# The second norm's factors move from the token tiles to the diagonals of the matrices that transpose them

## The chip, the cores and the metric

The kernel runs on one core of a Trainium2 chip. The metric is the device time of one execution in microseconds (us); the profiler also records the span of an execution, from its first to its last instruction. Five engines work side by side, each through its own list of instructions in order: PE (the tensor engine: matrix products), DVE, ACT and POOL (element-wise work) and SP (which here only issues DMA transfers). They wait for each other through semaphores. PE reads its operands from the on-chip memory SBUF and writes to PSUM, a small memory of eight banks from which DVE and ACT read. In the profile a product has two rows: PEld loads the stationary operand, PE streams the moving one.

## The reference, cut to what matters

One layer over 2048 latent tokens of 1024 channels, with 256 context tokens. Before each of its two halves the tokens are normed and modulated:

```python
def rmsnorm(x, g):
    y = xf * lax.rsqrt(jnp.mean(xf * xf, axis=-1, keepdims=True) + EPS) * g
def modulate(h, shift, scale):
    return h * (1.0 + scale) + shift

hx = modulate(rmsnorm(x, norm1_g), mx[:, :, 0], mx[:, :, 1])     # first norm
ux = hx @ w_in                                                   # mixer: FNet and HGRN2 branches
yx = merge_branches(ux, hgrn_readout(ux, ox, ...), w_a, w_b, w_out)
x = x + mx[:, :, 2] * yx
h2 = modulate(rmsnorm(x, norm2_g), mx[:, :, 3], mx[:, :, 4])     # second norm
x = x + mx[:, :, 5] * conv_ffn(h2, ffn_up, conv_w, conv_b, ffn_down, rows, cols)
return rmsnorm(x, final_g)
```

The norm's factor, 1 over the root of the mean square, is one number per token. Gain, scale and shift are one number per channel.

## The kernel before, in words

**Tiling.** Tokens are worked in four blocks (n = 0 to 3) of 512, each as four tiles (i = 0 to 3) of 128 tokens on the partitions by 1024 channels. The matrix products want the channels on the partitions, so a normed block is transposed in eight pieces (k = 0 to 7) of 128 channels: for each piece four transposes of 128x128, one for each token tile, fill one PSUM tile `pt` of 128x512. That is a "group of four" in what follows. Products are made in fp32 accuracy from three fast ones: an operand is split in `hi` (rounded to the format fp32r) and `lo` (the rest), and L146 to L148 add hi*hi, hi*lo and lo*hi. A few products (the FNet transforms, the scans) take plain fp32 operands.

**The function that transposes.** `modulate_steps` (L432) goes through the pieces k. For each it issues the group of four on PE (L440), then three steps that empty the PSUM tile: DVE forms A*pt+B in `mt` (L442), ACT forms the same rounded to fp32r as `hi` (L443), and DVE or POOL subtracts them to give `lo` (L445). A and B hold gain, scale and shift per channel. It is called for the first norm (at the start, for four blocks of tokens and the context, which has two tiles) and for the second norm (blocks 0 to 3, called through `h2_block`). The PSUM tiles `pt` come from rotating buffers: six at the start (tags tp, at, o), two for blocks 0 to 2 of the second norm, four for block 3.

**The norm's factors.** ACT squares and sums a token tile (L423, L962), DVE makes the factor `rs` in a chain of ten tiny instructions (L964, L125 to L129), and then DVE multiplies the token tiles by it: in place, four instructions of 128x1024 (L429 at the start, L970 in `h2_block`). Block 2 of the second norm is different: its tokens have been written to DRAM and come back in pieces `xc` of four 128x128 tiles (`reload_steps`, L972), and DVE multiplies each piece (L988) before it is transposed.

**What goes on around the second norm (phase 2, L844).** For each block n, `branches` makes eight output tiles j: for each j twelve products (four k by three) with w_a, then twelve with w_b, each set in one of two PSUM buffers `pj`, which DVE multiplies by a gate tile `gt` (L898). The two are added (L901), rounded by ACT (L902), and the rest is taken by DVE (L905). `out_proj` multiplies by w_out and adds the residual (L951, L952), and `h2_block` prepares the second norm of this block. Its eight groups of transposes are handed over as a generator and issued in between the next block's `branches` (none behind the tiles j = 0 and 1, one behind each of the next four, two behind the last two), so that block n is transposed while block n+1 is merged. Block 3 has no next one: its transposes stand among the first products of the up-projection (phase 3, `z`, L146 to L148). The gate tiles come from DRAM by SP (L880) in five rotating buffers of 128x512, two for each j, loaded one j ahead.

**Phase 3 and the end.** 44 up-projections with a 3x3 convolution on DVE and POOL, then the down-projection by a seven-product scheme (L1147 to L1149). There `ss` is a small tile of sums for the final norm, and behind it in the same SBUF pool lie the tiles `w`, `r0` and `r1`, into which weights and activations stream.

**What sets the order.** The program is written with tiles and pools, and a scheduler orders the instructions of each engine at compile time with its own estimate of how long each one takes. So another kind of instruction can also shift its neighbours.

Of the kernel before, what the change touches and what calls it, by code (L numbers as in the profile page):

```python
# [17 lines left out]
F32 = mybir.dt.float32  # L18
# [8 lines left out]
P = 128  # L27
# [4 lines left out]
TB = 512  # L32
KD = D // P
# [3 lines left out]
MUL, ADD, SUB = ALU.mult, ALU.add, ALU.subtract  # L37
# [57 lines left out]
class Layer:  # L95
# [335 lines left out]

    def modulate_steps(self, pool, xs, A, B, hi, lo, tags, every, bufs=2, k0=0, nk=KD):  # L432

# [3 lines left out]
        for k in range(k0, k0 + nk):  # L437
            pt = self.ps.tile([P, TB], F32, name="pt", tag=tags[k % len(tags)])
            for i in range(n):
                nc.tensor.transpose(pt[:, i * P:(i + 1) * P], xs[i][:, (k - k0) * P:(k - k0 + 1) * P], self.eye)  # L440
            tmp = pool.tile([P, TB], F32, name="mt", tag="mt", bufs=bufs)
# [427 lines left out]
    def branches(self, p4, n, t_lo, t_hi, bg):  # L869
# [7 lines left out]
        def load_gates(j):  # L877
            gates[j] = [p4.tile([P, TB], F32, name=f"gt{b}", tag="gt", bufs=5) for b in range(2)]
            for b in range(2):
                nc.sync.dma_start(gates[j][b], (self.dGA if b == 0 else self.dGB)[j][n])  # L880
# [75 lines left out]
    def h2_block(self, p4, n, xs, slots, tags):  # L956
# [7 lines left out]
        nc.vector.tensor_scalar(vv, ss, 1.0 / D, EPS, op0=MUL, op1=ADD)  # L964
        rs = self.rsqrt(p4, vv, 4)
        hi, lo = self.h2[n] = [self.ph.tile([P, KD, TB], F32R, name=f"h2{n}{i}", tag=f"H{slots[i]}") for i in range(2)]
        if n == 2:
            return self.reload_steps(p4, rs, hi, lo, tags)
        for i in range(4):
            nc.vector.tensor_scalar(xs[i], xs[i], rs[:, i:i + 1], None, op0=MUL)  # L970
        return self.modulate_steps(self.p4b, xs, self.mod2_A, self.mod2_B, hi, lo, tags, 4)

    def reload_steps(self, p4, rs, hi, lo, tags):

# [10 lines left out]
        def steps():  # L985
            for k in range(KD):
                xc = pieces.pop(0)
                nc.vector.tensor_tensor(xc, xc, fap(rs, 0, [(1, 4), (0, P)]), op=MUL)  # L988
                xs = [xc[:, i, :] for i in range(4)]
                for _ in self.modulate_steps(self.p4b, xs, self.mod2_A, self.mod2_B, hi, lo, tags, 4, 2, k, 1):  # L990
                    pass
                if k + 2 < KD:
                    pieces.append(load(k + 2))
                yield
# [156 lines left out]
    def down(self, last, pools):  # L1151
# [4 lines left out]
        with ExitStack() as es:  # L1156
# [13 lines left out]
            fg = p6.tile([P, D], F32, name="fg")  # L1170
            ss = p6.tile([P, 2, 16], F32, name="ss")
            X = {}
# [127 lines left out]
```

## Time and profile before

| | us |
|---|---|
| median of three runs | 3076.26 |
| lowest, highest | 3072.92, 3078.34 |
| profiled execution, its own time | 3078.62 |
| profiled execution, its span | 3076.8 |
| PE busy (98% of the span) | 3017.8 |
| DVE busy (60%) | 1847.2 |
| POOL busy (35%) | 1065.1 |
| ACT busy (30%) | 923.0 |

Busy time counts each engine by itself. "Idle before" in the rows of a timeline is the time in which the engine had nothing running ahead of that instruction, with the instruction that ended the wait. Times in a timeline count from the span's start. A row of a timeline can hold several equal instructions (x4); its second number is the time from the first one's start to the last one's end. The granted clock (PEclk) is the share of full speed that the tensor engine was given in a stretch; over the whole profiled run it was 0.994.

### The profile page before, as it was taken

The page shows a single profiled execution, that of the slowest core. Times are in us where ns is not written, and L with a number is a line of the kernel's source. Part 1 is how long each engine was busy: PE and PEld are TensorE (multiplying, and loading weights), DVE is VectorE, ACT ScalarE, POOL GpSimd, SP SyncE. Part 2 cuts the span into 40 slices and gives each one's busy share as a digit, 9 for nine tenths or more (in the row PEclk, how much of TensorE's full clock was granted, in tenths as well). Part 3 has the DMA queues.
Part 4 walks back from the last instruction along what each step waited for, and adds up shares of the span by engine and source line. Part 5 has one row for each costly group of instructions (what it writes and reads, how often), then busy time and mean ns, then how long its engine had stood idle before and what let it go on. Part 6 is the DMA issues. An engine that isn't in the chain of part 4 may idle for free. (4 is left out here: it accounts for less than half of the span.)

```text
span 3076.8 us, 38641 instructions
## 1 busy us (share of the span) xinstructions
PE 3017.8 (98%) x14691; PEld 2507.9 (82%) x14691; DVE 1847.2 (60%) x2503; ACT 923.0 (30%) x1439; POOL 1065.1 (35%) x714
## 2 busy tenths in 40 slices
PE   8999999999999999999999999999999999999998
PEld 5977788888888888887777888888888888787876
DVE  6355544366666650256775777676767677664366
ACT  4322111233333331233443322333233323221122
POOL 2200101000000001234543566777677767401400
PEclk9999999999999999999999999999999999999999
DMA  6255555422333223555564344554455454898783
GB/s 251 86 170 175 183 170 162 149 93 94 102 107 102 94 76 103 177 190 189 186 210 136 118 140 142 166 172 163 148 164 180 145 162 163 309 389 283 226 304 133
DMA packets 314459, 516.25 MB, mean 168 GB/s; under 512 B 24267, under 2 KB 162338, under 8 KB 309922
## 3 DMA queue, kind: packets, MB, share of 16 engines
q1 hardware_dynamic: 289602, 428.77, 42.1%
q0 software_dynamic: 22368, 80.81, 7.5%
q10 hardware_dynamic: 2304, 4.20, 0.4%
q8 instruction: 116, 1.90, 0.3%
q14 instruction: 69, 0.57, 0.1%
HBM read 364.52 MB, written 149.16 MB: 167 GB/s over the span
## 5 line engine op out<-in xcount | busy, mean ns | idle before, releaser
L1062 DVE SCALAR_TENSOR_TENSOR ac<-z,cw,ac 128x1953 f32<-128x1953 f32 (+2 forms) x309 | 703.1, 2275 | 255.6 <-ACT be L1032 231.0
L146 PE MATMUL z<-h,w_up 128*128 128x512 f32 x1408 | 548.0, 389 | 0.0
L147 PE MATMUL z<-h,w_up 128*128 128x512 f32 x1408 | 548.0, 389 | 0.0
L148 PE MATMUL z<-h,w_up 128*128 128x512 f32 x1408 | 547.9, 389 | 0.0
L147 PEld LDWEIGHTS z<-h,w_up 128*128 128x128 f32 x1408 | 264.3, 188 | 54.9
L146 PEld LDWEIGHTS z<-h,w_up 128*128 128x128 f32 x1408 | 264.3, 188 | 54.7
L148 PEld LDWEIGHTS z<-h,w_up 128*128 128x128 f32 x1408 | 264.3, 188 | 54.7
L1037 POOL TENSOR_TENSOR ac<-ac,be 128x1984 f32<-128x1984 f32 x43 | 192.2, 4469 | 209.5 <-DVE ac L1062 209.4
L1029 ACT ACTIVATE ac<-z,vt,cw 128x2048 f32<-128x2048 f32 x44 | 90.9, 2067 | 454.4 <-PE z L148 454.4
L1147 PE MATMUL d<-w,g 128*128 128x512 f32 x528 | 209.5, 397 | 6.7 <-issue 3.0
L1149 PE MATMUL d<-w,g 128*128 128x512 f32 x528 | 208.4, 395 | 0.0
L1148 PE MATMUL d<-w,g 128*128 128x512 f32 x528 | 208.4, 395 | 0.0
L493 ACT ACTIVATE ev<-pj 128x512 f32<-128x512 f32 (+1 forms) x136 | 79.6, 585 | 369.1 <-PE pj L148 335.3
L102 ACT CAST g<-r 128x1024 fp32r<-128x1024 f32 x69 | 69.9, 1047 | 280.2 <-PE d L1149 113.3
L1136 POOL DMA_DIRECT2D w<-dW x69 | 37.4, 543 | 305.1 <-PE d L1149 275.3
L1138 DVE TENSOR_TENSOR r<-r,r 128x1024 f32<-128x1024 f32 x55 | 68.2, 1242 | 115.3 <-DMA r<-dZ 74.0
L787 PEld LDWEIGHTS pa<-bQ,bkc 128*128 128x128 f32 x896 | 120.6, 191 | 17.2 <-issue 10.8
L103 POOL TENSOR_TENSOR wab<-rw,wab 128x512 fp32r<-128x512 f32 x64 | 93.9, 1486 | 113.9 <-ACT wab L102 113.8
L787 PE MATMUL pa<-bQ,bkc 128*128 128x128 f32 x896 | 127.6, 286 | 1.3
L1147 PEld LDWEIGHTS d<-w,g 128*128 128x128 f32 x528 | 99.3, 188 | 35.0 <-DVE x L1214 6.8
L793 DVE COPY_PREDICATED bA<-mask,pa 128x512 f32<-128x512 uint8 x112 | 82.7, 738 | 71.6 <-PE pa L787 70.6
L781 ACT COPY bkc<-bK 128x512 f32<-128x512 f32 x112 | 74.2, 663 | 164.1 <-PE pa L787 95.2
(341 smaller groups left out, 6808.4 us busy)
## 6 DMA issues: line engine op xcount, KB each, us to landing
r<-dZ SPq DMA_DIRECT2D x124, 512.0 KB, 7.1
dW<-wsr POOLq DMA_DIRECT2D x77, 512.0 KB, 5.9
w<-dW POOLq DMA_DIRECT2D x69, 512.0 KB, 6.2
ws<-dV SPq DMA_DIRECT2D x132, 256.0 KB, 4.2
rw<-in_ffn_up_dram SPq DMA_DIRECT2D x88, 256.0 KB, 4.2
dZ<-ac SPq DMA_DIRECT2D x22, 1024.0 KB, 4.0
rw<-in_w_in_dram SPq DMA_DIRECT2D x72, 256.0 KB, 3.4
maw<-in_ada_w_dram SPq DMA_DIRECT2D x64, 256.0 KB, 3.1
```

The costliest lines, as they stand in the source:

```text
L103: (eng or self.nc.gpsimd).tensor_tensor(lo, raw, hi, op=SUB)
L146: self.nc.tensor.matmul(ps, lh, rh, start=start and i == 0, stop=False)
L147: self.nc.tensor.matmul(ps, lh, rl, start=False, stop=False)
L148: mm = self.nc.tensor.matmul(ps, ll, rh, start=False, stop=stop and i == last)
L787: mm = nc.tensor.matmul(pa[:, c], kc[:, c], fap(Q, w * P, [(2 * m, nw), (W + m, 2), (1, m)]), start=True, stop=True)
L793: v.copy_predicated(at.rearrange("p (w t) -> p w t", w=4), fap(self.mask, lv * P, [(0, 4), (1, P)]), pa.rearrange("p (w t) -> p w t", w=4))
L1029: self.centre = nc.scalar.activation(ac, z, AF.Identity, scale=self.cw[:, 4, jj:jj + 1], bias=self.v("cb", jj))
L1037: added = nc.gpsimd.tensor_tensor(ac[:, :SEQ - 64], ac[:, :SEQ - 64], be[:, 64:], op=ADD)
L1062: nc.vector.scalar_tensor_tensor(o, z3[:, r0 + dy:r1 + dy, c0 + dx:c1 + dx], self.cw[:, k, jj:jj + 1], o, op0=MUL, op1=ADD)
L1147: nc.tensor.matmul(acc, gh[:, t], wh, start=(k == 0), stop=False)
L1148: nc.tensor.matmul(acc, gh[:, t], wl, start=False, stop=False)
L1149: nc.tensor.matmul(acc, gl[:, t], wh, start=False, stop=(k == KH - 1))
```

## The change

For the second norm, the token tiles are no longer multiplied by the factors. Instead four diagonal matrices `dg` are made from the identity, one for each token tile, with the factors on the diagonal, and the step that transposes uses `dg` in the identity's place: the product of a tile (transposed) with a diagonal matrix is the transposed tile with each token's column scaled. [...] The buffer for `dg` (2 KB per partition) is taken from the gate tiles, which go from five buffers to four. The tile of sums `ss` of the end grows from 128 to 512 bytes per partition, with the same columns of it used.

```diff
--- before.py
+++ after.py
@@ -429,7 +429,7 @@
             nc.vector.tensor_scalar(xs[i], xs[i], rs[:, i:i + 1], None, op0=MUL)
         return xs
 
-    def modulate_steps(self, pool, xs, A, B, hi, lo, tags, every, bufs=2, k0=0, nk=KD):
+    def modulate_steps(self, pool, xs, A, B, hi, lo, tags, every, bufs=2, k0=0, nk=KD, dg=None):
 
 
         nc = self.nc
@@ -437,7 +437,8 @@
         for k in range(k0, k0 + nk):
             pt = self.ps.tile([P, TB], F32, name="pt", tag=tags[k % len(tags)])
             for i in range(n):
-                nc.tensor.transpose(pt[:, i * P:(i + 1) * P], xs[i][:, (k - k0) * P:(k - k0 + 1) * P], self.eye)
+                nc.tensor.matmul(pt[:, i * P:(i + 1) * P], xs[i][:, (k - k0) * P:(k - k0 + 1) * P],
+                                 dg[:, i, :] if dg else self.eye, start=True, stop=True)
             tmp = pool.tile([P, TB], F32, name="mt", tag="mt", bufs=bufs)
             nc.vector.tensor_scalar(tmp[:, :n * P], pt[:, :n * P], A[:, k:k + 1], B[:, k:k + 1], op0=MUL, op1=ADD)
             nc.scalar.activation(hi[:, k, :], pt[:, :n * P], AF.Identity, scale=A[:, k:k + 1], bias=B[:, k:k + 1])
@@ -875,7 +876,7 @@
         br, gates = self.br, {}
 
         def load_gates(j):
-            gates[j] = [p4.tile([P, TB], F32, name=f"gt{b}", tag="gt", bufs=5) for b in range(2)]
+            gates[j] = [p4.tile([P, TB], F32, name=f"gt{b}", tag="gt", bufs=4) for b in range(2)]
             for b in range(2):
                 nc.sync.dma_start(gates[j][b], (self.dGA if b == 0 else self.dGB)[j][n])
 
@@ -963,14 +964,15 @@
         vv = p4.tile([P, 4], F32, name="vv", tag="vv", bufs=2)
         nc.vector.tensor_scalar(vv, ss, 1.0 / D, EPS, op0=MUL, op1=ADD)
         rs = self.rsqrt(p4, vv, 4)
+        dg = p4.tile([P, 4, P], F32, name="dg", tag="dg", bufs=1)
+        for i in range(4):
+            nc.vector.tensor_scalar(dg[:, i, :], self.eye, rs[:, i:i + 1], None, op0=MUL)
         hi, lo = self.h2[n] = [self.ph.tile([P, KD, TB], F32R, name=f"h2{n}{i}", tag=f"H{slots[i]}") for i in range(2)]
         if n == 2:
-            return self.reload_steps(p4, rs, hi, lo, tags)
-        for i in range(4):
-            nc.vector.tensor_scalar(xs[i], xs[i], rs[:, i:i + 1], None, op0=MUL)
-        return self.modulate_steps(self.p4b, xs, self.mod2_A, self.mod2_B, hi, lo, tags, 4)
-
-    def reload_steps(self, p4, rs, hi, lo, tags):
+            return self.reload_steps(p4, dg, hi, lo, tags)
+        return self.modulate_steps(self.p4b, xs, self.mod2_A, self.mod2_B, hi, lo, tags, 4, dg=dg)
+
+    def reload_steps(self, p4, dg, hi, lo, tags):
 
         nc = self.nc
 
@@ -985,9 +987,8 @@
         def steps():
             for k in range(KD):
                 xc = pieces.pop(0)
-                nc.vector.tensor_tensor(xc, xc, fap(rs, 0, [(1, 4), (0, P)]), op=MUL)
                 xs = [xc[:, i, :] for i in range(4)]
-                for _ in self.modulate_steps(self.p4b, xs, self.mod2_A, self.mod2_B, hi, lo, tags, 4, 2, k, 1):
+                for _ in self.modulate_steps(self.p4b, xs, self.mod2_A, self.mod2_B, hi, lo, tags, 4, 2, k, 1, dg):
                     pass
                 if k + 2 < KD:
                     pieces.append(load(k + 2))
@@ -1168,7 +1169,7 @@
                 q.__exit__(None, None, None)
             p6 = self.p6 = es.enter_context(tc.tile_pool(name="p6", bufs=1, reuse_waits="tile"))
             fg = p6.tile([P, D], F32, name="fg")
-            ss = p6.tile([P, 2, 16], F32, name="ss")
+            ss = p6.tile([P, 2, 64], F32, name="ss")
             X = {}
 
             def load_quarter(th, c, tag):
```

What this does to the order of the instructions, at three places. (Line numbers of the changed kernel are one higher from L441 on: its L443, L899, L902 and L906 are L442, L898, L901 and L905 of before. Its L969 makes `dg`.)

**DVE, where block 0's second norm ends while block 1 is merged.** `x` is the block's token tile, `gt` a gate tile, `pj` the PSUM tile of a set of twelve products, `ml` the low part of the merged result. Before:

```order
L970 TENSOR_SCALAR x_11420<-x_11420,rs_y 128x1024 x4
L898 TENSOR_TENSOR gt_11814<-pj,gt_11814 128x512
L901 TENSOR_TENSOR gt_11813<-gt_11813,gt_11814 128x512
L898 TENSOR_TENSOR gt_11856<-pj,gt_11856 128x512
L905 TENSOR_TENSOR ml_11798<-gt_11813,mh_11799 128x512
L898 TENSOR_TENSOR gt_11857<-pj,gt_11857 128x512
L442 TENSOR_SCALAR mt<-pt,mod_A,mod_B 128x512
```

And in the changed kernel:

```order
L969 TENSOR_SCALAR dg<-eye,rs_y 128x128 x4
L899 TENSOR_TENSOR gt_11815<-pj,gt_11815 128x512
L902 TENSOR_TENSOR gt_11814<-gt_11814,gt_11815 128x512
L906 TENSOR_TENSOR ml_11799<-gt_11814,mh_11800 128x512
L899 TENSOR_TENSOR gt_11857<-pj,gt_11857 128x512
L899 TENSOR_TENSOR gt_11858<-pj,gt_11858 128x512
L902 TENSOR_TENSOR gt_11857<-gt_11857,gt_11858 128x512
```

The four large multiplications have given way to four small ones at the same place, and the step that takes the low part (L905, now L906) has moved ahead of the next eviction of `pj`. PE's order is the same as before here, and both are alike where block 1 ends.

**PE, where block 2's second norm begins while block 3 is merged.** `wab` are the weights of the branches, `y` their inputs, `xc` a piece of tokens that has come back from DRAM. Before:

```order
L146 MATMUL pj<-y_13356,wab 128x512
L147 MATMUL pj<-y_13356,wab 128x512
L148 MATMUL pj<-y_13356,wab 128x512
L146 MATMUL pj<-y_13206,wab 128x512
L147 MATMUL pj<-y_13206,wab 128x512
L148 MATMUL pj<-y_13206,wab 128x512
L440 MATMUL pt<-eye,xc 128x128 x4
```

And in the changed kernel:

```order
L146 MATMUL pj<-y_13358,wab 128x512
L147 MATMUL pj<-y_13358,wab 128x512
L148 MATMUL pj<-y_13358,wab 128x512
L440 MATMUL pt<-dg,xc 128x128 x4
L146 MATMUL pj<-y_13208,wab 128x512
L147 MATMUL pj<-y_13208,wab 128x512
L148 MATMUL pj<-y_13208,wab 128x512
```

The first group of four has moved three products ahead, to the end of a set of twelve.

**PE, where block 3's second norm is transposed among the first products of the up-projection.** Here `x_13876` to `x_13879` (one less each in the changed kernel) are the block's four token tiles. Before:

```order
L146 MATMUL z<-h_12596,w_up_14300 128x512
L147 MATMUL z<-h_12597,w_up_14300 128x512
L148 MATMUL z<-h_12596,w_up_14300 128x512
L440 MATMUL pt<-eye,x_13876 128x128 x4
L146 MATMUL z<-h_12596,w_up_14300 128x512
L440 MATMUL pt<-eye,x_13877 128x128 x4
L147 MATMUL z<-h_12597,w_up_14300 128x512
L440 MATMUL pt<-eye,x_13878 128x128 x4
L148 MATMUL z<-h_12596,w_up_14300 128x512
```

And in the changed kernel, where the same four rows of L440 come eight times in all before the next product of `z`:

```order
L146 MATMUL z<-h_12602,w_up_14300 128x512
L440 MATMUL pt<-dg,x_13875 128x128
L440 MATMUL pt<-dg,x_13876 128x128
L440 MATMUL pt<-dg,x_13877 128x128
L440 MATMUL pt<-dg,x_13878 128x128
L440 MATMUL pt<-dg,x_13875 128x128
L440 MATMUL pt<-dg,x_13876 128x128
L440 MATMUL pt<-dg,x_13877 128x128
L440 MATMUL pt<-dg,x_13878 128x128
```

The 32 transposes stood in groups with products of `z` between them, tile by tile; now they stand in one run, piece by piece, two products of `z` earlier. At the start, too, the groups are drawn together: 26 and 32 in a run for the first two blocks, where before there were 18 and 24 with the rest among the products.

## The prediction

> **What bounds the kernel now.** I read the page first, then the busy time by stages, then PE's timeline.
>
> ```profile
> span 3076.8 us, 38641 instructions
> PE 3017.8 (98%) x14691; PEld 2507.9 (82%) x14691; DVE 1847.2 (60%) x2503; ACT 923.0 (30%) x1439; POOL 1065.1 (35%) x714
> ```
>
> A busy share of 98% does not yet say that PE is the bound everywhere. The stages in which the changed instructions stand are these (start and end, length, busy time of PE, PEld, DVE, ACT, POOL with counts, granted clock, DMA):
>
> ```profile
> 36.00:60.00 24.00, 21.41 (x145) 19.40 (x146) 18.40 (x37) 16.10 (x28) 9.48 (x7) 0.86 0.40 147
> 80.00:140.00 60.00, 60.00 (x505) 59.88 (x503) 22.48 (x45) 19.40 (x31) 15.16 (x12) 1.00 0.23 79
> 1285.00:1400.00 115.00, 110.20 (x479) 90.20 (x478) 67.41 (x93) 39.95 (x69) 49.84 (x33) 0.99 0.63 206
> 1660.00:1700.00 40.00, 37.83 (x182) 30.71 (x181) 23.43 (x36) 16.73 (x22) 13.91 (x11) 1.00 0.38 128
> 2690.00:3040.00 350.00, 344.74 (x1470) 275.35 (x1469) 188.06 (x235) 78.98 (x111) 59.00 (x71) 1.00 0.82 284
> ```
>
> From 80 to 140 us PE never rests: what is added to it there lengthens the run one for one. In the other stages it rests 2 to 5 us, and the question is what ends those rests. The first stage is different (a lower clock, DVE busy three quarters), and I treat it by itself.
>
> **The price of a product in place of a transpose.** L440 has 128 + 112 + 32 = 272 transposes, in 68 groups of four (the context's eight pieces have two each). All of them change, since the new instruction serves the first norm too. For a plain fp32 product of the same shape the trace has L787: by the code 448 products (four for each of seven levels, four blocks and four heads), and 896 records.
>
> ```profile
> L440 PE MATMUL pt<-eye,x x128: 270/273/476, 32.0 to 1682.1; 128*128 128x128 f32 x128
> L440 PE MATMUL pt<-eye,xt x112: 270/272/332, 58.3 to 155.8; 128*128 128x128 f32 x112
> L440 PE MATMUL pt<-eye,xc x32: 270/272/421, 1581.1 to 1619.0; 128*128 128x128 f32 x32
> ...
> L787 PE MATMUL pa<-bQ,bkc x896: 270/275/358, 607.4 to 1144.0; 128*128 128x128 f32 x180
> ```
>
> (The last row's end, "x180", belongs to its first form.) So a transpose is one record and a plain product two, each of the same 270 to 275 ns. But records overlap, so the price is the distance between starts:
>
> ```profile
> 625.92 1.05 PE L787 MATMUL pa<-bQ,bkc 128*128 128x128 f32 x8
> 626.73 0.47 PE L146 MATMUL pj<-hT,w_Q 128*128 128x512 f32 x1
> ...
> 628.20 0.60 PE L653 MATMUL pt<-eye,bK 128*128 128x128 f32 x4
> 628.55 0.48 PE L146 MATMUL pj<-hT,w_Q 128*128 128x512 f32 x1
> ...
> 633.00 0.38 PE L820 MATMUL po<-bV,bA 128*128 128x128 f32 x2
> ...
> 634.33 0.39 PE L820 MATMUL po<-bV,bA 128*128 128x128 f32 x2
> ...
> 103.21 3.76 PE L440 MATMUL pt<-eye,xt 128*128 128x128 f32 x32
> 106.72 0.36 PE L376 MATMUL pj<-fw,hT 128*128 128x256 f32 x1
> ```
>
> Four products among others take 626.73 - 625.92 = 0.81 us, four transposes 0.35: 0.46 us more for a group. In a long run 32 transposes take 3.51 us, 0.110 each; between the two rows of L820 lie six products, 1.33 us, 0.222 each (0.111 a record): 32 cost 7.10, 3.6 us more. Both ways it is one more record of 0.11 us for each transpose. [...]
>
> **The terms.**
>
> 1. First norm, blocks 1 to 3, and the context. Three runs of 32 at 3.6 us: **+10.8**. The context's 16: 16 x 0.111 = **+1.8**. Cover: none, PE is full from 80 to 140 us.
>
> 2. First norm, block 0. Here the trace shows slow transposes, and a PE that waits for the steps behind them:
>
> ```profile
> 42.00:44.00 2.00, 2.00 (x12) 2.00 (x11) 1.85 (x5) 1.95 (x4) 1.37 (x2) 0.50 1.10 334
> ...
> 40.29 4.04 PE L440 MATMUL pt<-eye,x 128*128 128x128 f32 x18
> ...
> 44.05 0.40 PE L376 MATMUL pj<-fw,hT 128*128 128x256 f32 x1
> ...
> 46.90 0.50 PE L378 MATMUL pj<-fw,hT 128*128 128x256 f32 x2 [0.52 <-POOL hT L445]
> ```
>
> At a clock of 0.50 a transpose takes 3.76/18 = 0.21 us, so a product 0.42. The run of 26 costs 10.9 us if the clock stays there and 5.8 at full clock. PE would start the products behind it at 46 to 51 us and not at 44.05, but those wait for the steps that empty `pt` anyway: PE rests 24.00 - 21.41 = 2.6 us in this stage. So between nothing (-0.5, should the waits fall together better) and +4.5; I take **+1.0**, since the cover of 2.6 us nearly meets a run that ends at about 47.5 with the clock raised half way through. [...]
>
> 3. Second norm, blocks 0 to 2: 24 groups among products, 24 x 0.46 = **+11.0**.
>
> 4. Block ends 0 and 1 (the gain). DVE's four multiplications stand ahead of the eviction that PE waits for:
>
> ```profile
> 1387.41 2.74 DVE L970 TENSOR_SCALAR x<-x,rs_y 128x1024 f32<-128x1024 f32 x4
> 1387.90 0.39 PE L147 MATMUL pj<-y,wab 128*128 128x512 f32 x1
> 1388.13 0.39 PE L148 MATMUL pj<-y,wab 128*128 128x512 f32 x1
> 1390.07 0.69 DVE L898 TENSOR_TENSOR gt<-pj,gt 128x512 f32<-128x512 f32 x1
> 1390.90 0.47 PE L146 MATMUL pj<-y,wab 128*128 128x512 f32 x1 [2.38 <-DVE gt L898]
> ...
> 1394.88 1.05 PE L440 MATMUL pt<-eye,x 128*128 128x128 f32 x4
> ...
> L550 DVE TENSOR_SCALAR fE<-fE 128x128 f32<-128x128 f32 x12 | 2.6, 216 | 0.0
> ...
> 1487.90 0.70 PE L146 MATMUL pj<-y,wab 128*128 128x512 f32 x1 [2.40 <-DVE gt L898]
> ...
> 1492.33 0.60 PE L440 MATMUL pt<-eye,x 128*128 128x128 f32 x4
> ```
>
> `dg` takes four times L550's 216 ns, 0.87 us, in place of 2.66 (to 1390.07): PE goes on 1.8 us earlier. After the stop, the twelve products up to the transposes take 3.98 us and 4.43 at the next block end, though twelve at the distance before it (1387.90 to 1388.13: 0.23) take 2.8: the clock had dropped. If a rest of 2.4 - 1.8 = 0.6 us no longer drops it, that is 1.2 and 1.6 more. So the gain is between 2 x 1.8 = 3.6 and 6.4; I take **-6.4**, since the rest that remains is a quarter of the one that did it. L905 now stands ahead of an eviction and waits for ACT; its place has more than 1 us to spare by then, so I cost it at nothing.
>
> 5. Block end 2. The stop comes from the factor's chain itself, and the first group of four now stands at it:
>
> ```profile
> 1579.83 0.16 DVE L129 SCALAR_TENSOR_TENSOR rs_y<-rs_t,rs_y 128x4 f32<-128x4 f32 x1
> 1579.87 0.53 PE L146 MATMUL pj<-y,wab 128*128 128x512 f32 x1 [2.01 <-DVE rs_t L128]
> ...
> 1581.06 1.05 PE L440 MATMUL pt<-eye,xc 128*128 128x128 f32 x4
> ```
>
> PE must wait for `dg`, whose first matrix is there at 1579.99 + 0.22 = 1580.2 and last at 1580.9, before it may go on with products that it began at 1579.87. Between +0.3 and +2; I take **+1.0** beyond the group's own 0.46. The eight multiplications L988 that fall away free DVE where PE didn't wait for it.
>
> 6. Second norm, block 3: eight groups, 8 x 0.46 = 3.7. In one run, each piece from the fifth on waits for one of four `pt` to be emptied, with no products of `z` between. Before, PE waited too:
>
> ```profile
> 1673.43 0.66 PE L440 MATMUL pt<-eye,x 128*128 128x128 f32 x4 [1.10 <-DVE x L970]
> ...
> 1680.52 0.66 PE L440 MATMUL pt<-eye,x 128*128 128x128 f32 x4 [0.72 <-ACT h L443]
> ```
>
> The rests were 40.00 - 37.83 = 2.2 us; I reckon 1.0 for the first `dg` and 1.5 for the last two pieces, 2.5 (bounds 1 and 4). So 3.7 + 0.3 = **+4.0**.
>
> 7. The fifth gate buffer. A load's wait for a free buffer now comes one step earlier in the pairs, and SP issues in order, so the weights (L115) queue behind it. The tightest pair had:
>
> ```profile
> 1605.87 0.34 SPq L880 DMA_DIRECT2D gt<-dGA  x1
> ...
> 1611.83 0.68 DVE L898 TENSOR_TENSOR gt<-pj,gt 128x512 f32<-128x512 f32 x1
> ...
> DMA to landing us min/median/max: 2.6/3.2/4.7
> ```
>
> With four buffers the load at 1605.87 is the one needed at 1611.83, 6.0 us later, and it lands in at most 4.7: **0**, up to +3 over all blocks if it doesn't.
>
> 8. The tile of sums moves `w`, `r0` and `r1` by 384 bytes and nothing in any engine's order. PE is busy 344.74 of 350 us there: **0**, within 1 either way.
>
> Sum: 10.8 + 1.8 + 1.0 + 11.0 - 6.4 + 1.0 + 4.0 = **+23.2**. The profiled execution took 3078.6 us (its span and 1.8 around it) and would take 3101.8; against the median of 3076.3, 2.3 lower, that is **3099.5**.
>
> **The rivals.**
>
> *Covered costs (3092 to 3095).* Block 0 hides its products entirely, block end 2 costs nothing and no longer drops the clock either: 1.0 + 1.0 + about 1.6 (as at block end 1) less, and up to 2 of block 3's rests: +17 to +19. For it: the rests are there. Against it: PE has to rest at just these places.
>
> *New waits (3105 to 3110).* Most of these come together: the clock drops at block ends 0 and 1 all the same (+2.8), block 0 runs at the low clock (+3.5), gates come late (+3), block 3's run waits longer (+1.5): up to +34. For it: the run of 32 without products in between, and the clock of 0.50 that is seen in block 0. Against it: each needs its own mishap.
>
> *Four passes (3160).* If a product with these operands took the time of four records and not of two, 272 x 2 x 0.11 = 60 us more would come on top. Against it: every plain product of this shape in the trace, whatever its operands, has two. [...]
>
> *One record (3071, not slower).* If the product with a diagonal or identity went through in one record, as the transpose does, terms 1, 2, 3 and the 3.7 of 6 would vanish and the gain of 4 stay: -6.4 + 1.0 + 0.3 = -5.1. The vanishing terms are 28.3 us at 0.11 a record, so it decides where the second record costs less than 0.11 x 5.1/28.3 = 0.02 us. For it: the change adds no instruction to PE's order. Against it: L787.
>
> **How the numbers follow.** My forecast 0.70, covered costs 0.10, new waits 0.13, four passes 0.03, one record 0.04. The forecast's own range is 3094 to 3106; to leave out no more than 2 in 10 it must take in most of the cases beside it: 3091 to 3110. A measurement of this kernel tells about 0.2% (6 us) from no change. All cases but the last are slower by more than that: 0.95, with a little kept back for a cover that I don't see; the last lies at the edge: 0.03 for no change, 0.02 for faster.
>
> **What would show it.** L440 with 544 records, groups of four at 0.81 us, runs of 32 at 7.1; no stop over 1 us behind `dg` at block ends 0 and 1, and a granted clock of 1.00 there; at block end 2 a wait of PE for `dg`; from 1700 us on everything as before, only later. I am wrong if L440 has 272 records, if PE rested elsewhere for as long as its new records take, or if the down-projection changes its length by more than 1 us.

## The result and the profile after

The changed kernel took **3094.3 us** (median; 3094.1 to 3094.7) against 3077.3 us of the kernel before: a ratio of **1.0060** with a 95% interval of 1.0048 to 1.0072, 17 us or 0.6% slower. A second set of times, with other runs of the kernel before (after_again below), gave 1.0057 (1.0042 to 1.0072). The prediction was 3099.5 us, with a range of 3091 to 3110. The profiled execution has a span of 3092.3 us, 15.5 us more than before.

The page of the changed kernel begins:

```profile
span 3092.3 us, 39172 instructions
PE 3034.3 (98%) x14963; PEld 2537.5 (82%) x14963; DVE 1830.4 (59%) x2499; ACT 924.2 (30%) x1439; POOL 1072.9 (35%) x714
```

PE is busy 16.5 us longer, DVE 16.8 us less. The instructions of L440 in the changed kernel:

```profile
L440 PE MATMUL pt<-eye,xt x224: 270/275/348, 59.2 to 167.8; 128*128 128x128 f32 x112
L440 PE MATMUL pt<-dg,x x192: 270/275/377, 1395.8 to 1693.3; 128*128 128x128 f32 x192
L440 PE MATMUL pt<-eye,x x64: 275/275/582, 32.2 to 48.6; 128*128 128x128 f32 x64
L440 PE MATMUL pt<-dg,xc x64: 270/275/377, 1589.0 to 1631.3; 128*128 128x128 f32 x64
...
  DVE dg L969: 8.1, 4
```

224 + 192 + 64 + 64 = 544 records for 272 products, two each. Their price, in a run and in a group among other products (start, length, instruction):

```profile
111.11 7.30 PE L440 MATMUL pt<-eye,xt 128*128 128x128 f32 x64
118.17 0.37 PE L376 MATMUL pj<-fw,hT 128*128 128x256 f32 x1
...
1395.79 1.05 PE L440 MATMUL pt<-dg,x 128*128 128x128 f32 x8
1396.60 0.48 PE L146 MATMUL pj<-y,wab 128*128 128x512 f32 x1
```

A run of 32 products takes 118.17 - 111.11 = 7.06 us (forecast 7.10), a group of four 0.81 us (forecast 0.81). So the price of a single product was right to a hundredth. What is left to explain is why terms that add up to 23 came out as 17.

For that, both profiles are cut at the same PE instructions: the first product of L598 (L599 in the changed kernel), the first with `y,wab`, the 33rd of L146 with `z<-h,w_up`, and the one that ends the up-projection but for its last columns. Busy time by stages (columns as in the prediction), before:

```profile
0.00:172.26 172.26, 158.42 (x1080) 132.13 (x1081) 86.73 (x184) 70.34 (x116) 46.74 (x44) 0.97 0.47 168
172.26:1284.73 1112.47, 1098.11 (x5878) 933.35 (x5877) 569.23 (x1300) 297.73 (x652) 92.06 (x70) 1.00 0.39 126
1284.73:1690.91 406.18, 392.64 (x1761) 321.74 (x1760) 256.50 (x352) 150.80 (x251) 176.30 (x122) 0.99 0.58 188
...
2621.15:3076.80 455.65, 438.42 (x1873) 350.41 (x1871) 253.74 (x369) 105.32 (x148) 90.22 (x95) 0.99 0.79 275
```

and after:

```profile
0.00:183.67 183.67, 172.61 (x1218) 148.05 (x1219) 86.60 (x181) 70.58 (x115) 45.38 (x44) 0.97 0.45 158
183.67:1289.67 1106.00, 1094.34 (x5884) 930.64 (x5882) 568.88 (x1303) 298.67 (x653) 92.54 (x70) 1.00 0.39 127
1289.67:1706.13 416.46, 403.79 (x1890) 335.37 (x1888) 240.78 (x348) 150.69 (x251) 184.73 (x122) 1.00 0.57 186
...
2636.37:3092.30 455.93, 433.36 (x1873) 352.91 (x1871) 253.21 (x369) 105.57 (x148) 90.01 (x95) 0.98 0.78 274
```

The first norm costs 183.67 - 172.26 = 11.4 us (forecast 13.6, terms 1 and 2), the second 416.46 - 406.18 = 10.3 us (forecast 9.6, terms 3 to 6). But 6.5 us come back between 172 and 1284 us, where no instruction was changed. That was the first thing to test.

### The profile page after: what moved, and what is told of

Its sections match the earlier page's. It is cut to its first block, busy times and chain, and to the rows that moved or that the text cites. A ratio compares the mean times of both kernels' runs of the same rounds, so it can differ in the third digit from the quotient of the medians.

```text
span 3092.3 us, 39172 instructions
## 1 busy us (share of the span) xinstructions
PE 3034.3 (98%) x14963; PEld 2537.5 (82%) x14963; DVE 1830.4 (59%) x2499; ACT 924.2 (30%) x1439; POOL 1072.9 (35%) x714
## 5 line engine op out<-in xcount | busy, mean ns | idle before, releaser
L146 PE MATMUL z<-h,w_up 128*128 128x512 f32 x1408 | 547.7, 389 | 0.0
L146 PEld LDWEIGHTS z<-h,w_up 128*128 128x128 f32 x1408 | 264.4, 188 | 54.6
L103 POOL TENSOR_TENSOR wab<-rw,wab 128x512 fp32r<-128x512 f32 x64 | 100.2, 1585 | 113.1 <-ACT wab L102 113.1
L788 PEld LDWEIGHTS pa<-bQ,bkc 128*128 128x128 f32 x896 | 120.7, 191 | 16.8 <-issue 10.4
```

The source lines that it names most:

```text
L103: (eng or self.nc.gpsimd).tensor_tensor(lo, raw, hi, op=SUB)
L146: self.nc.tensor.matmul(ps, lh, rh, start=start and i == 0, stop=False)
L788: mm = nc.tensor.matmul(pa[:, c], kc[:, c], fap(Q, w * P, [(2 * m, nw), (W + m, 2), (1, m)]), start=True, stop=True)
```

## The experiments

Each ratio is against runs of the kernel before on the same chip, with its 95% interval; the clock and the stages are from one profile of each. The edits are shortened, some to a single line. Two theories stood against each other at the start: **R**, that a delay at the start is taken back between 160 and 410 us, and **S**, the prediction's, that PE is full and each microsecond added lengthens the run.

**First norm alone** (first_only). The kernel before with

```diff
-    nc.tensor.transpose(pt[:, i * P:(i + 1) * P], x, self.eye)
+    nc.tensor.matmul(pt[:, i * P:(i + 1) * P], x, self.eye, start=True, stop=True)   # first norm only
```

> Only the first norm's transposes (blocks 0 to 3 and the context) become plain products with the identity; the second norm, the gate buffers and the tile of sums stay as before. What is added to PE up to 170 us is the same as in the changed kernel, 11.4 us by its trace (start of the first product on L598). Theory R (part of a delay at the start is taken back between 160 and 410 us, where DVE and loads set PE's rests): +5 against before, 4 to 7. Theory S (the prediction's: PE is full, each added us lengthens the run): +11.8, 10.5 to 13. In the trace, R shows +11 at L598 and about +5 at 420 us.

Measured: 1.0025 (1.0012 to 1.0037), +4 to +11 us. In its trace L598 begins at 183.9 us and the block ends' stage at 1293.0, 8.3 us behind before's 1284.7 and not 5: R is not borne out in the place where it was to be seen. The time doesn't decide: by means it is +8.0, between R's 4 to 7 and S's 10.5 to 13, and the profiled execution (3093.7 us) was the second slowest of nine.

**Second norm alone** (second_only). The changed kernel with

```diff
+    if dg: nc.tensor.matmul(pt[...], x, dg[:, i, :], start=True, stop=True)
+    else:  nc.tensor.transpose(pt[...], x, self.eye)
```

> The changed kernel with the first norm's transposes as before: only the second norm's groups are products, with the factors on the diagonals. By the prediction's terms 3 to 6: +9.6 against before. By the trace of the changed kernel, whose delay grew from 4.9 us at the first product of the block ends' stage to 15.2 us behind block 3: +10.3. So 8 to 12 by both; with first_only it tells whether the two halves add up to the whole (+17): 17 - 10 = 7 is left for the first norm by R, and 9.6 + 11.8 = 21.4 would be the whole by S.

Measured: 1.0022 (1.0012 to 1.0031), +4 to +10 us; by means +6.4, less than the 8 to 12 that both sums gave. Its trace brought the surprise: up to 1284 us it has the instructions of the kernel before, and yet it reached the first `wab` product at 1276.7 us, 8.0 us ahead of before's profile. So executions of one and the same code differ there by more than the effect that R was made up for.

**The delay without the products** (dummy_early). The kernel before, with the transposes of the first norm's blocks 1 to 3 issued twice:

```diff
-    for i in range(n):
+    for i in [i for i in range(n) for _ in range(times)]:      # times=2 for blocks 1 to 3
         nc.tensor.transpose(pt[:, i * P:(i + 1) * P], ...)
```

> The kernel before, with each of the 96 transposes of the first norm's blocks 1 to 3 issued twice into the same place: 96 x 0.11 = 10.5 us of PE work more, without one plain product. R says that it is the delay that is taken back, whatever makes it: +4 to +6. S: +10.5. If the products themselves do it (by what they do to the clock, say), then +10.5 here and +5 in first_only.

Measured: 1.0025 (1.0016 to 1.0035), +5 to +11 us, by means +6.4: it reaches from R's numbers to S's, and is no verdict by itself. L598 begins at 179.5 us, 8.2 us behind the mean of the eight profiles with the old start (171.3 us), and not 10.5: a part of the doubled run lay in rests. Taken together, the stage from L598 to the first `wab` product is 1.5 us shorter in the six profiles with a late start (this one and the five with the first norm's products) than in the eight without, 1107.7 for 1109.2 us. That is what is left of R's 6.5.

**The same delay late** (dummy_late). The kernel before with

```diff
+    if jj == 4:
+        for _ in range(96): nc.tensor.transpose(z[:, :P], self.eye, self.eye)
```

> The kernel before, with 96 transposes of the identity more, in one run, ahead of the up-projection's fifth column tile (about 1750 us), where PE is busy 988.5 of 990 us. R and S agree here: +10.5, 9 to 12, since no rest of PE's follows before the down-projection. If it is clearly less, delays are taken back in the down-projection too, and the early give-back is nothing special.

Measured: 1.0033 (1.0020 to 1.0045); the up-projection's stage of 930.24 us became 940.77, 10.5 us longer to the tenth. Where PE had no rests, work added was work lost, as S has it.

**The tile of sums alone** (sums64).

```diff
-    ss = p6.tile([P, 2, 16], F32, name="ss")
+    ss = p6.tile([P, 2, 64], F32, name="ss")
```

> The kernel before with the tile of sums of 512 bytes alone. The prediction (term 8): nothing is changed in any engine's order, 0 within 1 us. Theory A (the addresses count): in the changed kernel and in second_only, which both have the larger tile, the products of the down-projection start 0.227 us apart (37 of them from 2775.65 to 2784.04), before 0.233 (47 from 2759.79 to 2770.76). On 1656 such products with operands from the tiles behind it that is 10.9 us of PE's time; but from the last column tiles of the up-projection to the end the two took 455.6 and 455.9 us and the four with the smaller tile 455.7 to 461.7, so a part goes into new rests: -3 for the whole run, -1 to -7.

Measured: 1.0006 (0.9995 to 1.0017): no difference that can be told. But the products did become faster. In the kernel before, 45 of them lie between these two rows of PE's timeline:

```profile
2759.79 0.40 PE L1149 MATMUL d<-w,g 128*128 128x512 f32 x1
...
2770.29 0.39 PE L1149 MATMUL d<-w,g 128*128 128x512 f32 x1
```

and in the changed kernel 36 between these:

```profile
2775.65 0.39 PE L1150 MATMUL d<-w,g 128*128 128x512 f32 x1
...
2783.81 0.39 PE L1150 MATMUL d<-w,g 128*128 128x512 f32 x1
```

10.50/45 = 0.2333 us from one to the next before, 8.16/36 = 0.2267 after. Over the whole stage the median distance is 0.227 us in the five profiles with the larger tile (sums64 among them) and 0.232 in the nine with the smaller. Theory A's mechanism is there, but nearly nothing of its 10.9 us arrives: in the last stage of the two profiles above PE's busy time falls by 5.1 us and its rests grow by 5.3. What the products saved there, the rests took up.

**The gate buffers alone** (gates4).

```diff
-    gates[j] = [p4.tile(..., tag="gt", bufs=5) for b in range(2)]
+    gates[j] = [p4.tile(..., tag="gt", bufs=4) for b in range(2)]
```

> The kernel before with four gate buffers in place of five, and nothing else. The prediction (term 7): 0. Rival: in the trace of the changed kernel PE waited 1.25 and 0.62 us for weights behind block end 2, whose load was issued behind gates and pieces of tokens that waited for buffers; if the fourth buffer does it, +2 to +4 here, and PE's waits for wab are seen in the trace; if it was the later transposes, 0 here.

Measured: 1.0006 (0.9994 to 1.0018). PE's waits in the second norm's stages of gates4 (place, cause, us in total, times, longest):

```profile
PE pj L146 <- ACT wab L102: 1.7, 1, 1.7
PE pj L148 <- POOL wab L103: 1.3, 1, 1.3
```

and the same in the changed kernel:

```profile
PE pj L146 <- ACT wab L102: 1.2, 1, 1.2
PE pj L148 <- POOL wab L103: 0.6, 1, 0.6
```

Waits for `wab` of 1.1 to 4.0 us stand in all five profiles with four buffers (this one, the changed kernel's two, second_only and after_sums16), and in none of those with five but the two below that load ACT. The rival is right about the waits (the weights' load stands on SP behind gates and pieces that wait for a buffer); about the time (by means +1.9, for its +2 to +4) it stays below what these runs can tell. The profiled execution, 3090.4 us, was the slowest of the twelve.

**The fifth buffer put back** (after_gt5). The changed kernel with

```diff
-    gt: bufs=4;  dg = p4.tile([P, 4, P], F32, name="dg", tag="dg", bufs=1)
+    gt: bufs=5;  dg = self.p4b.tile([P, 4, P], F32, name="dg", tag="m2", bufs=1)
```

> The changed kernel with its fifth gate buffer back (the diagonals lie in the tile m2 instead, which is free then). By the prediction (term 7) the same as the changed kernel, +15 to +17 against before. If the fourth buffer made the two waits for weights behind block end 2 (1.9 us), those are gone and the whole is +13 to +15.

Measured: 1.0054 (1.0040 to 1.0068). The waits for `wab` are gone; the time lies inside the changed kernel's interval.

**The gain alone** (act_scale). The kernel before, with DVE rid of the four multiplications without any product:

```diff
+    if n < 2: nc.scalar.activation(xs[i], xs[i], AF.Copy, scale=rs[:, i:i + 1])
+    else:
         nc.vector.tensor_scalar(xs[i], xs[i], rs[:, i:i + 1], None, op0=MUL)
```

> The kernel before with the four multiplications of blocks 0 and 1 on ACT in place of DVE, so that the evictions that PE waits for come earlier and no product costs more: term 4 alone. By the prediction -3.6 to -6.4. Rival: what is left of the stop is made by the chain of small operations ahead of the multiplications, of which three or four take 1.2 us and not 0.16 when POOL is at work; then the stop shrinks by less, and whether the clock still drops behind it is decided by how the rest falls (1.90 us of rest and more within one stretch of 3.41 us dropped it in every trace so far, 1.80 and less did not): 0 to -4.

Measured: **0.9983** (0.9973 to 0.9994), -2 to -8 us; by means -4.5. PE and ACT at block end 0 of act_scale:

```profile
1377.80 0.47 PE L146 MATMUL pj<-y,wab 128*128 128x512 f32 x1 [1.67 <-DVE rs_t L127]
```
```profile
1378.15 4.27 ACT L971 ACTIVATE x<-x,rs_y 128x1024 f32<-128x1024 f32 x4 [3.76 <-DVE rs_y L129]
```

ACT had stood idle for 3.76 us and multiplies now, off PE's path. The stop of 1.67 us that is left stands behind the chain of small operations, and it was there before too (below); the one behind the multiplications, 2.38 us before, is gone. So the rival was right about the chain, and term 4 about the multiplications: the time allows both forecasts, the stages of the two block ends came to -5.5 (below). The change pays a second record for each of the second norm's 128 products (544 records less the first norm's 224 + 64 are 256), 128 x 0.11 = 14 us, for what ACT does off PE's path.

**More of it** (act_more). act_scale with

```diff
-    nc.vector.tensor_tensor(xc, xc, fap(rs, 0, [(1, 4), (0, P)]), op=MUL)
+    for i in range(4): nc.scalar.activation(xc[:, i, :], xc[:, i, :], AF.Copy, scale=rs[:, i:i + 1])
```

and the last of block 3's four multiplications on ACT.

> act_scale, with more of DVE's multiplications on ACT: block 2's pieces (four of 128 columns for each piece, in place of one on DVE) and the last of block 3's four. In act_scale PE waited 3.1 us once for a piece that DVE had to multiply and 1.1 us for block 3's tokens. If those waits go: -3 more, -7 to -8 against before. Rival: ACT, which must cast weights and evict pt there too, becomes late in its turn, and it is -4.5 as act_scale or less.

Measured: 0.9982 (0.9973 to 0.9990), by means -5.3. The rival came true: PE's one long wait for a piece is now one for ACT (2.7 us in place of 3.1), and the 1.1 us for block 3's tokens stayed. By its ratio it is the fastest kernel of the study, but not measurably faster than act_scale.

**The diagonals alone** (diag_only). The kernel before with `dg` in the second norm only, five gate buffers, and the small tile of sums.

> The kernel before with the second norm's factors on diagonals and nothing else: first norm by transposes, five gate buffers (the diagonals lie in the tile m2), tile of sums as before. Terms 3 to 6 alone. By the prediction +9.6. By the stage from the first wab product to the 33rd of the up-projection, which took 406.2 to 409.8 us in five kernels with the second norm as before and 416.1 to 421.0 in three with the diagonals: +10.4. second_only, with the larger tile of sums, had +6.4 by its mean; if that tile gives 3.5, +10 here, if not, +6 to +7.

Measured: 1.0022 (1.0014 to 1.0031), +4 to +10 us; by means +6.6. That is the same as second_only, with the small tile of sums in place of the large and five gate buffers in place of four. The forecast of +9.6 lies at the interval's end.

**Once more, and with the small tile** (after_again, the changed kernel itself; after_sums16, the same with `ss` of 16).

> The changed kernel once more, beside the next two on one chip, for a profile of another execution of the same instructions and for more times. Against before +15 to +19. If differences of several us between executions come from where a stretch of 3.41 us of lowered clock begins, its stages differ from the first profile's by 1.7 us at a time, at rests of about 1.9 us, and nowhere else.

> The changed kernel with the tile of sums as before. By the profiles, from the last up-projection products to the end kernels with the larger tile took 455.6 to 457.1 us (four) and with the smaller 455.7 to 467.1 (six), means 3.5 us apart; by the times of sums64 the larger tile is worth nothing (+1.2, within 1.3). Theory A (the faster products are worth a part of their 10.9 us in the run's time): +3.5 over after_again. The prediction (term 8, and the times of sums64): within 1 of it. The products of the down-projection should be 0.233 us apart again.

Measured: 1.0057 (1.0042 to 1.0072) and 1.0065 (1.0051 to 1.0079). The stages of after_again differ from the first profile's by +3.7 us up to the first `wab` product, -2.5 at block end 1, +1.3 at block end 2 and +1.8 at the end. In each of the first three lies one stretch of lowered clock more or less, 1.7 us by an estimate (half of its 3.41 us at a clock of 0.50); the rest is not the clock's (up to the first `wab` product PE rested 14.0 us for 11.7), so the expectation held in part only. By medians the small tile is 3.1 us slower, in the sense of theory A, but the intervals overlap, and sums64 alone showed no gain. The products are 0.232 us apart again. What the larger tile is worth stays open between 0 and about 3 us.

## Why the prediction came out as it did

With fourteen profiles each stage can be read from several executions of the same instructions. Lengths in us, each from the starts of the PE instructions named above: mean, and in brackets the lowest and highest. Block end 0 reaches from the first `wab` product to the first product of block 1's `out_proj`, block end 1 from there to that of block 2, block end 2 from there to the first up-projection, block 3 from there to the 33rd of it. Left out are dummy_early in the first two rows and act_scale and act_more in the next four; the up-projection, 930.24 us in all but dummy_late, has no row.

| stage | as before | as changed | difference | forecast |
|---|---|---|---|---|
| start to L598 | 171.3 (169.7 to 172.6), 8 profiles | 183.1 (182.0 to 183.9), 5 | +11.8 | +13.6 (terms 1 and 2) |
| L598 to first `wab` | 1109.2 (1106.6 to 1112.5), 8 | 1107.9 (1106.0 to 1109.7), 5 | -1.3 | 0 |
| block end 0 | 140.1 (138.8 to 141.4), 6 | 140.7 (140.4 to 141.3), 6 | +0.6 | +0.5 |
| block end 1 | 96.6 (95.4 to 98.0), 6 | 100.3 (98.3 to 101.8), 6 | +3.7 | +0.5 |
| block end 2 | 142.9 (139.5 to 144.7), 6 | 144.7 (142.4 to 146.7), 6 | +1.9 | +4.7 |
| block 3 | 28.3, 6 | 31.2, 6 | +2.9 | +4.0 |
| last columns to the end, by the tile of sums | 459.1 (455.5 to 467.1), 9 | 456.6 (455.6 to 457.8), 5 | -2.5 | 0 |

The differences add up to +17.1, and the time moved by 17. That they meet so closely is in part luck: the times don't confirm the last row's -2.5 (sums64 by means: +1.2), and single stages spread by several us.

**Terms 1 and 2, the first norm: the price right, the cover missed.** The step that failed is "Cover: none, PE is full from 80 to 140 us". That row holds only the third of the three runs; the first two begin at 58.26 and 75.68 us. Between the end of block 0's run and the end of the second one (44.05 to 80.10 us) PE rested 3.1 us before and 1.0 in the changed kernel, so 2.1 us were covered; the third run came in whole (+3.6). The three runs together came to +7.2 for 10.8 in the mean; what the cover of 2.1 doesn't explain of that stays open. Block 0's +1.0, with a clock assumed to rise half way through (it was 0.50 up to 45.36 us, up to 44.14 before), came to +4.6 (the first product behind its run begins at 48.63 us for 44.05), the upper end that was given. All in all +11.8 of 13.6 is there at L598. The context's sixteen products stand ahead of L598 too, but their 1.8 us don't show there: six products of `pj<-hT,w_F`, about 0.23 us each, have moved behind L598 (53 stood ahead of it, 47 now), and the next stage has them. The clock was no help, as the changed kernel's first stage shows:

```profile
36.00:60.00 24.00, 22.96 (x164) 21.77 (x164) 17.70 (x36) 16.65 (x29) 9.48 (x8) 0.86 0.37 135
```

0.86 as before, and PE's rests fell from 2.6 to 1.0 us: of the cover that was counted on, 1.6 us was used. At the first `wab` product 3.1 us less than forecast arrive. Part of it is that the clock drops less often behind L598 (below): thirteen times in the eight profiles as before, twice in the five as changed, 2.8 and 0.7 us in the mean. Five of the thirteen followed a rest of PE's near 200 us, which was 1.8 to 3.1 us as before and 1.6 to 2.0 as changed. Why it is shorter there stays open; the later start alone doesn't do it (dummy_early: 3.1 us, and no drop). Theory R, which had 6.5 us here, had compared two single executions; before's profile happened to be the slowest of eight in this stage. The spread makes the 3.1 uncertain by about 1.

**Term 4, the gain: the stop that it prices went as forecast, but it was not the only one.** PE stops twice at each block end of the kernel before. The second stop, 2.38 us behind the four multiplications, is the one in the prediction. The first stands 5.4 us earlier; there the eviction that PE waits for comes behind a part of the factor's chain:

```profile
1385.52 0.47 PE L146 MATMUL pj<-y,wab 128*128 128x512 f32 x1 [1.67 <-DVE gt L898]
```

Both in the changed kernel, with the step that makes `dg` between them:

```profile
1389.44 0.47 PE L146 MATMUL pj<-y,wab 128*128 128x512 f32 x1 [1.69 <-DVE gt L899]
...
1391.33 0.88 DVE L969 TENSOR_SCALAR dg<-eye,rs_y 128x128 f32<-128x128 f32 x4
...
1392.95 0.47 PE L146 MATMUL pj<-y,wab 128*128 128x512 f32 x1 [0.50 <-DVE gt L899]
```

The second stop fell from 2.38 to 0.50 us (0.50 to 0.53 in all six profiles with diagonals; 0.6 was reckoned), so "no stop over 1 us behind `dg`" came true. In the mean PE's rests fell from 4.4 to 2.3 us at block end 0, and the clock, which had dropped there in three of six profiles, dropped in none. Behind `dg` no stop over 1 us is left at block end 1 either, but there the rests stayed (4.1 and 3.9 us), since the first stop grew to 2.8 to 3.3 us in five of the six profiles, and the clock dropped in four of them, for three of six before. The step that failed is "a rest of 2.4 - 1.8 = 0.6 us" as all that remains: the stop behind the factor's chain is in no term. So the gain of 6.4 came to 3.1 at block end 0 and to nothing at block end 1 (the differences of the table less 3.7 for the eight groups). The chain was slow where POOL was at work. DVE at block end 1 of the changed kernel:

```profile
1484.35 1.26 DVE L128 SCALAR_TENSOR_TENSOR rs_t<-rs_t,vv 128x4 f32<-128x4 f32 x1
1485.65 1.22 DVE L129 SCALAR_TENSOR_TENSOR rs_y<-rs_t,rs_y 128x4 f32<-128x4 f32 x1
...
1487.10 0.16 DVE L128 SCALAR_TENSOR_TENSOR rs_t<-rs_t,vv 128x4 f32<-128x4 f32 x1
...
1487.78 1.22 DVE L129 SCALAR_TENSOR_TENSOR rs_y<-rs_t,rs_y 128x4 f32<-128x4 f32 x1
1488.92 0.68 DVE L899 TENSOR_TENSOR gt<-pj,gt 128x512 f32<-128x512 f32 x1
```

its POOL:

```profile
1484.30 2.55 POOL L103 TENSOR_TENSOR wab<-rw,wab 128x512 fp32r<-128x512 f32 x2 [4.40 <-ACT wab L102]
1487.67 2.54 POOL L103 TENSOR_TENSOR wab<-rw,wab 128x512 fp32r<-128x512 f32 x2 [0.82 <-ACT wab L102]
```

and its PE:

```profile
1489.75 0.77 PE L146 MATMUL pj<-y,wab 128*128 128x512 f32 x1 [2.85 <-DVE gt L899]
```

In these rows an operation on four numbers for each partition took 0.16 us, and 1.22 to 1.26 us in the three that ran while POOL was in a subtraction of its pairs (2.54 and 2.55 us). In the kernel before, POOL's second pair began at 1481.62 us and DVE's L129 at 1481.61, a hundredth ahead of it, and took 0.15. Here POOL began at 1487.67, 0.11 us ahead of L129, which then took 1.22 us and stood ahead of the eviction: measured from POOL's start the two are 0.12 us apart. In five of the six profiles with diagonals this operation took 1.22 or 1.23 us at block end 1, and of those without them first_only has a stop as long there (2.88 us). In act_scale and act_more, which also free DVE, it took 0.15, and there both block ends are shorter (by 2.6 and 2.9 us in the mean of the two): term 4's -6.4 with no product to pay came to -5.5.

**Term 5, block end 2: the wait as forecast, the cost less.** The first group of the changed kernel waits as foretold:

```profile
1589.01 1.16 PE L440 MATMUL pt<-dg,xc 128*128 128x128 f32 x8 [2.52 <-DVE dg L969]
```

2.52 us, for 2.01 before. But "The eight multiplications L988 that fall away free DVE where PE didn't wait for it" failed, and one profile could not have shown it. DVE and PE behind block end 2 of sums64, which has the second norm of before:

```profile
1615.03 1.48 DVE L988 TENSOR_TENSOR xc<-xc,rs_y 128x512 f32<-128x512 f32 x1
```
```profile
1616.61 1.09 PE L440 MATMUL pt<-eye,xc 128*128 128x128 f32 x4 [2.26 <-issue]
```

The view names no releaser, but DVE's L988 on this piece ends at 1616.51 us, 0.1 us ahead of the group. PE stands 2.3 to 2.6 us before this group in five of the six profiles with the old second norm; only in before's own it was 0.49. The diagonals take this wait away, and the clock of 0.50 that followed it in four of the five.

**Term 6, block 3:** +2.9 for +4.0; the rests fell from 2.2 to 1.4 us and did not grow by 0.3.

**Term 7, the gates:** the time as forecast as far as these runs can tell, but the step "it lands in at most 4.7" looked at the gate's own load. What came late were the weights that stand behind it on SP (PE waited 1.2 and 0.6 us for them in the changed kernel), as the prediction's sentence on SP's order says and its sum left out.

**Term 8, the tile of sums: near zero, for a wrong reason.** It moves nothing "in any engine's order", true, but the products that read the tiles behind it start 2 to 3% closer together (0.227 us for 0.232 in medians). It came to nearly nothing because PE's rests in that stage grew as its work shrank. In the pair of profiles the stage's length changed by 0.3 us, within the bound of 1 that was set; in the means of the table it is -2.5 (1.0 of it from gates4's 467.1 alone), which the times don't confirm.

**The rivals.** The time lies at the lower edge of the forecast's own range and inside that of "covered costs" (whose parts, 3.6 to 5.6 off 23.2, make +17.6 to +19.6 where it says +17 to +19). That is no proof of that rival: block 0 cost more than forecast, and what was covered at block end 2 (-2.8 against the forecast) and in block 3 (-1.1) was nearly paid back at block end 1 (+3.2). The other 5.6 us between 23 and 17 are the 3.1 us up to the first `wab` product and the unconfirmed 2.5 of the last row. "One record" and "four passes" are out by L440's 544 records at 0.11 us. Of "new waits" the dropped clock at block end 1 came, in four profiles of six, and the waits for weights behind block end 2.

## To carry to other kernels

A product that replaces a transpose is cheap to price and was priced right; what was not is the other side: of two stops only the one that it was to remove was looked at. Before an engine's work is moved onto the one that is full, look for one that is idle at that very moment: here ACT, 3.8 us idle, gave the gain (ratio 0.9983) without the 14 us of second records. And compare a stage over several executions before explaining a few microseconds in it: the unchanged stage from L598 to the first `wab` product differed by up to 5.9 us between executions of the same instructions.

## What the runs showed that was not expected

**The clock's drops lay on a grid.** In all fourteen profiles, between 36 and 3060 us, every stretch of halved clock (0.50) began at a multiple of 3.413 us plus one offset per execution (3.18 us in before's profile, 0.98 in that of the changed kernel), and lasted 3.41 us or a multiple of it; in before's profile the stretches at 37.31 and 1580.14 us begin 452 times 3.413 us apart. From 60 us on, the drops went with how long PE had rested within the cell ahead. Two cells of the kernel before (start and end, length, PE's busy time first, granted clock third from the end):

```profile
1388.99:1392.40 3.41, 1.50 (x7) 1.27 (x8) 3.29 (x6) 0.62 (x1) 0.00 (x0) 1.00 0.71 214
1392.40:1395.81 3.41, 3.41 (x12) 2.72 (x11) 1.15 (x2) 0.64 (x2) 0.00 (x0) 0.50 0.54 154
```

and four of the changed kernel:

```profile
1584.77:1588.18 3.41, 1.73 (x8) 1.11 (x6) 3.23 (x8) 0.00 (x0) 1.58 (x2) 1.00 0.52 154
1588.18:1591.59 3.41, 2.58 (x15) 2.32 (x16) 3.31 (x11) 0.62 (x1) 0.00 (x0) 1.00 0.30 94
...
1485.78:1489.19 3.41, 1.12 (x5) 0.57 (x4) 3.34 (x6) 1.14 (x2) 2.59 (x3) 1.00 0.14 39
1489.19:1492.60 3.41, 2.85 (x7) 2.30 (x8) 3.27 (x10) 0.00 (x0) 1.02 (x1) 0.50 0.95 288
```

Before, the clock was halved in the cell behind one with 1.91 us of rest. In the changed kernel the rest of 2.52 us at block end 2 fell into two cells, 1.68 and 0.83 us, and the clock stayed at 1.00; behind 2.29 us in one cell at block end 1 it was 0.50. Over all profiles between 60 and 3050 us, cells at full clock with less than 1.66 us of rest were never followed by a drop, cells with 1.97 us or more always were, and between the two both happen. Behind cells at halved clock the line lay lower: with up to 0.56 us of rest the clock came back, with 0.70 us or more it stayed down. At the start rest isn't all: the cell ahead of before's first low stretch here (33.90 to 37.31 us) had none, and 1.9 us of it went to products of one column (L345); what counts there the runs don't show. At a clock of 0.50 the products of `pj` behind before's block end 1 started 0.43 us apart, for 0.23 at 1.00, and the transposes at the start 0.21, for 0.11; so a drop of 3.41 us costs 1.6 to 1.7 us, an estimate from these distances. The offset differs from execution to execution, and a rest of about 2 us costs that or nothing by how it falls (2.25 to 2.64 us ahead of block 2's transposes did in four profiles and, split into 0.93 and 1.32, didn't in gates4). By that estimate this is one source of the spread of 3069 to 3086 us between runs of the kernel before. The prediction's clock terms (1.2 and 1.6 us) are what a drop cost in one execution; at each of the two block ends it came in three of six, so the six executions put such a term at about half.

**The clock rose behind transposes as it did behind products.** The cell of the kernel before that ends its first low stretch, filled by the transposes of block 0, and the one of the changed kernel, filled by its products:

```profile
40.72:44.14 3.42, 3.42 (x19) 3.42 (x17) 3.27 (x8) 2.31 (x4) 1.51 (x2) 0.50 1.08 361
```
```profile
41.94:45.36 3.42, 3.42 (x18) 3.42 (x17) 2.36 (x5) 3.15 (x5) 2.52 (x3) 0.50 0.80 236
```

Behind both the clock is 1.00. In the cell ahead of each PE was busy throughout as well, and the clock stayed at 0.50 in both kernels; the small transposes of L352 took 1.1 and 0.8 us of it.

**A small DVE operation took about eight times its length**, 1.22 to 1.26 us for 0.16, where POOL was in a subtraction; the rows are above.

**The place of a tile in memory moved the pace of the products that read it**: 384 bytes further on, 0.2267 us for 0.2333 at the place shown, in medians 0.227 for 0.232.
